# Moving the marks behind which a gathered expert sum may run, in a two-layer backbone with product-key experts

## The chip, the cores and the metric

The kernel runs on one core of one Trainium2 chip. The metric is device time in microseconds (us) of one execution, as the median of several runs. The engines are called PE (TensorE, the matrix engine), PEld (its weight loads), DVE (VectorE), ACT (ScalarE), POOL (GpSimd) and SP (the queue that issues most loads).

## What is computed

Two layers run over one block of 128 context tokens and two blocks of 128 latent tokens. Each layer has a mixer (two kinds of attention and a gated MLP) and then PEER, a layer of 128 x 128 = 16384 experts of one neuron each. This is the part that matters here, cut from the reference:

```python
def one(xb):                                   # 128 tokens
    ...
    top, pos = lax.top_k(cand, PEER_TOPK)      # 8 heads x 16 experts for each token
    idx = jnp.take_along_axis(cidx, pos, axis=-1)
    g = jax.nn.softmax(top.astype(jnp.float32), axis=-1).astype(xb.dtype)
    a = jax.nn.gelu(jnp.einsum('thkd,td->thk', u_tab[idx], xb))
    return jnp.einsum('thk,thkd->td', g * a, v_tab[idx])
```

A token picks 128 experts. For each it needs one row of the table U (1024 numbers; a dot product with the token) and one row of the table V (1024 numbers; added with a weight).

## The kernel before, in words

The kernel computes PEER in two ways at once. For the 256 **latent** tokens it goes densely through both tables on PE. For the 128 **context** tokens it gathers rows. The two share DVE, the DMA engines and the time.

**The dense stages**, one after the other in each layer, for the latent tokens:

- A: `a_step` 0 to 31. Each loads two U tiles (128 experts each, 512 KB), splits most of them into a high and a low part (high on ACT, line 846; low on DVE, line 847, `ulo`), multiplies them with the tokens (line 852) and writes the activations into a large array AR.
- W, the first gate half: 32 `w_step`s. Each builds one-hot matrices for 8 tokens on DVE (lines 876, 878, 883) or ACT (872, 874), multiplies them on PE (line 890, `psW`) and scales AR with the product on DVE (line 897). After every second one there is an `a_step` (32 to 47).
- B: sixteen times one `o_step` (0 to 15) and one `a_step` (48 to 63). An `o_step` loads two V tiles, splits AR (ACT line 906, DVE line 907, `pp`) and mostly also the V tiles (ACT line 915, DVE line 916, `vlo`), and adds the products to four accumulators on PE (line 926, `acc`).
- X, the second gate half: 32 `w_step`s for the other 64 groups of experts, and after every second one an `o_step` (16 to 31); of these, ten of sixteen don't split their V tiles.
- O: `o_step` 32 to 63, all split. Each needs the gates of X for all its tokens, so the first waits for the last write to AR in X.

`U` and `V` tiles come through a ring of six buffers, loaded by SP in program order (line 157); the split parts have two buffers each (pool `w`, `WB = 2`).

**The gathered steps** for the context tokens: 256 in each layer, made in `ctx_gathers`. Steps 0 to 127 are `u_step`s: POOL gathers 128 rows of U with an indirect DMA (line 686, 512 KB, four buffers `gt` in turn), and DVE multiplies and sums them (line 692). Steps 128 to 255 are `v_step`s: POOL gathers rows of V, and DVE adds them to a running sum (line 703; step 128 itself is on line 701). When the last one is done, `ctx_close` normalises the context tokens. In layer 0 their next layer begins there (projection `psic`, line 262); in layer 1 they are written out (line 719).

**Order.** The program is written in the order above, but a scheduler places the instructions of each engine by a simulated timeline and by priority, earlier code first; the order on each engine is then fixed in the program. The gathered steps are written last, so they fill what is free. They would be placed too early where that hurts, so each one is put behind a mark with `tc.issue_after`: its DVE instruction may not be placed ahead of the marked DVE instruction. The gather on POOL has no mark; it waits for its buffer, which DVE frees four steps earlier. Marks are collected by stage: L (top-16 lists of the router), A, W, B, X and O. A mark of A or B is the DVE split of one U tile (line 847), a mark of W or X the first one-hot comparison of one `w_step` (line 878), a mark of O the split of one V tile (line 916). There are 32 marks in L, 40 in A, 32 in W, 32 in B, 32 in X and 64 in O, in each layer. `RATES` says how many steps one mark lets go, `N0` how many steps at the start have no mark:

```python
hold = []
for k, r in RATES[l].items():
    ms = marks[k]
    n = int(len(ms) * r + 0.5)
    hold += [ms[int(i / r)] for i in range(n)]
for j, f in enumerate(ctx_gathers(l, pk)):
    if j < N0[l] or j - N0[l] >= len(hold):
        f()
    else:
        with tc.issue_after(hold[j - N0[l]].ins):
            f()
```

So before the change, in layer 0, 50 steps are free, 8 are let go on L, 56 on A, none on W, 64 on B, 32 on X, and the remaining 46 on O; in layer 1 these are 60, 4, 49, 0, 76, 16 and 51.

Of the kernel before, what the change touches and what calls it, by code (L numbers as in the profile page):

```python
# [45 lines left out]
def tile_fn(ctx: ExitStack, tc, A, outs):  # L46
# [703 lines left out]
    for l in range(DEPTH):  # L750
# [45 lines left out]
        with ExitStack() as es_:  # L796
# [199 lines left out]
# [3 lines that stand above are left out]
# [21 lines left out]
BK = [dict(m=1,s=2,t=2,o=1)]*2  # L1020
PK2 = 'mm'
CQ = 0
RATES = [{'L':0.25,'A':1.4,'W':0.01,'B':2,'X':1,'O':2.125}, {'L':0.125,'A':1.225,'W':0.01,'B':2.375,'X':0.5,'O':2.625}]
N0 = [50,60]
MB = 5
ORD1 = 'paollllllllllllll'
# [96 lines left out]
```

## Time and profile before

| what | us |
|---|---|
| median of 3 runs | 2407.3 (2402.37 to 2410.01) |
| the profiled execution | 2407.9 |
| its span in the trace | 2406.1 |
| PE busy | 2260.6 (94%) |
| DVE busy | 1904.6 (79%) |
| ACT busy | 1115.2 (46%) |
| POOL busy | 697.7 (29%) |
| gathered steps on DVE, lines 692 and 703 | 309.5 and 325.5 |

The span is what the trace covers from the first to the last instruction; the execution's time has a little around it. Busy shares are averages over stages with different limits, so the stage must be looked at before a share means something. Times within the trace count from the start of the span. In this execution the stage B of layer 0 runs from about 725 to 905 us, X to about 1045, O to about 1238; in layer 1 B runs from about 1890 to 2077, X to about 2214 and O to about 2390.

### The profile page before, as it was taken

What the parts mean: (1) busy time and instruction counts of PE and PEld (TensorE: products, weight loads), DVE (VectorE), ACT (ScalarE), POOL (GpSimd) and SP (SyncE); (2) the same over time, 40 slices, a digit from 0 to 9 for tenths busy, and PEclk for the clock granted to TensorE, in tenths of its full rate; (3) what the DMA queues carried; (4) which work ended last, traced back from release to release, by engine and by line L of the source; (5) the groups of instructions that cost most, each with busy time, mean ns of one, the idle gap of its engine ahead of it and who ended that gap; (6) DMA issues with size and microseconds to landing.
All of it is one profiled execution on the core that took longest, in us unless ns stands there. A gap on an engine that the chain in (4) does not pass through costs nothing.

```text
span 2406.1 us, 41658 instructions
## 1 busy us (share of the span) xinstructions
PE 2260.6 (94%) x15660; PEld 1914.5 (80%) x15660; DVE 1904.6 (79%) x3942; ACT 1115.2 (46%) x2084; POOL 697.7 (29%) x523
## 2 busy tenths in 40 slices
PE   6999889999999999999989996989999999998997
PEld 5686469999998995667778785889999889855886
DVE  3157579996898888898863468899879888899987
ACT  3324532442785445444445553134348744444444
POOL 0000233454004433464200003435530143344630
PEclk8999989999999999999999998999999999998998
DMA  9967889999658999999863355989985599987994
GB/s 331 322 193 265 336 322 348 324 358 350 219 159 295 360 332 347 328 352 374 299 213 113 120 158 196 325 313 349 363 320 159 188 374 346 333 309 270 395 364 147
DMA packets 196314, 696.05 MB, mean 289 GB/s; under 512 B 22992, under 2 KB 27408, under 8 KB 196112
## 3 DMA queue, kind: packets, MB, share of 16 engines
q1 hardware_dynamic: 110016, 398.52, 46.7%
q0 software_dynamic: 74736, 272.14, 31.1%
q10 hardware_dynamic: 11360, 22.73, 2.8%
q8 instruction: 123, 2.02, 0.3%
q14 instruction: 79, 0.65, 0.1%
HBM read 689.14 MB, written 4.16 MB: 288 GB/s over the span
## 4 chain that ended last, share of the span: by engine, by line
PE 32%; DVE 8%; issue 8%; DMA 2%; POOL 1%; ACT 1%; DVEq 0%; ACTq 0%; POOLq 0%
PE acc L926 18%; PE psA L852 6%; DVE gt L692 2%; PE psil L262 2%; DMA gt<-in_peer_u_dram,ids 1%; POOL gt L686 1%; PE psqp L561 1%; PE psic L262 1%; DVE ulo L847 1%; PE psoc L522 1%; PE pssl L421 1%; DMA wic<-in_w_in_dram 1%; PE psW L890 0%; DVE idx L550 0%; DVE rep L548 0%
## 5 line engine op out<-in xcount | busy, mean ns | idle before, releaser
L686 POOL DMA_INDIRECT gt<-in_peer_u_dram,ids x256 | 325.3, 1271 | 1185.6 <-DVE gt L692 478.4
L686 POOL DMA_INDIRECT gt<-in_peer_v_dram,ids x256 | 368.0, 1438 | 464.0 <-DVE acc L703 434.7
L926 PE MATMUL acc<-vhi,pp 128*128 128x512 f32 x1728 | 441.9, 398 | 15.6 <-ACT pp L906 9.4
L852 PE MATMUL psA<-h2hi,uhi 128*128 128x256 f32 x1664 | 416.2, 287 | 5.1 <-ACT uhi L846 5.1
L852 PE MATMUL psA<-h2lo,uhi 128*128 128x256 f32 x1664 | 411.3, 284 | 0.0
L926 PEld LDWEIGHTS acc<-vhi,pp 128*128 128x128 f32 x1728 | 326.1, 191 | 86.3 <-ACT pp L906 10.0
L915 ACT ACTIVATE vhi<-v 128x1024 fp32r<-128x1024 f32 x216 | 228.7, 1060 | 274.0 <-PE acc L926 161.2
L692 DVE SCALAR_TENSOR_TENSOR gt<-gt,h2c 128x1024 f32<-128x1024 f32 x256 | 309.5, 1216 | 28.0 <-DMA gt<-in_peer_u_dram,ids 27.9
L703 DVE SCALAR_TENSOR_TENSOR acc<-gt,wcol,acc 128x1024 f32<-128x1024 f32 x254 | 325.5, 1282 | 6.2 <-DMA gt<-in_peer_v_dram,ids 5.2
L846 ACT ACTIVATE uhi<-u 128x1024 fp32r<-128x1024 f32 x208 | 220.0, 1058 | 230.2 <-PE psA L852 107.5
L852 PEld LDWEIGHTS psA<-h2hi,uhi 128*128 128x128 f32 x1664 | 319.7, 192 | 7.9 <-ACT uhi L846 5.7
L852 PEld LDWEIGHTS psA<-h2lo,uhi 128*128 128x128 f32 x1664 | 320.0, 192 | 2.1
L847 DVE TENSOR_TENSOR ulo<-u,uhi 128x1024 fp32r<-128x1024 f32 x208 | 254.3, 1223 | 79.9 <-ACT uhi L846 74.7
L916 DVE TENSOR_TENSOR vlo<-v,vhi 128x1024 fp32r<-128x1024 f32 x216 | 263.6, 1223 | 52.6 <-ACT vhi L915 47.7
L852 PE MATMUL psA<-h2hi,ulo 128*128 128x256 f32 x1664 | 239.4, 286 | 1.0 <-DVE ulo L847 0.8
L926 PE MATMUL acc<-vlo,pp 128*128 128x512 f32 x864 | 234.3, 392 | 1.5 <-DVE vlo L916 1.4
L852 PEld LDWEIGHTS psA<-h2hi,ulo 128*128 128x128 f32 x1664 | 216.2, 192 | 3.0 <-DVE ulo L847 1.6
L872 ACT ACTIVATE e<-iota,nid 128x128 f16<-128x128 f16 x512 | 158.9, 426 | 112.1 <-PE psW L890 112.1
L926 PEld LDWEIGHTS acc<-vlo,pp 128*128 128x128 f32 x864 | 162.3, 189 | 35.8 <-DVE vlo L916 2.5
L852 PE MATMUL psA<-h2T,u 128*128 128x256 f32 x768 | 171.8, 379 | 0.0
L852 PEld LDWEIGHTS psA<-h2T,u 128*128 128x128 f32 x768 | 143.1, 190 | 18.1
L926 PE MATMUL acc<-v,AR 128*128 128x512 f32 x320 | 143.6, 599 | 0.0
(437 smaller groups left out, 3039.9 us busy)
## 6 DMA issues: line engine op xcount, KB each, us to landing
u<-in_peer_uT_dram SPq DMA_DIRECT2D x256, 512.0 KB, 6.0
v<-in_peer_v_dram SPq DMA_DIRECT2D x256, 512.0 KB, 6.0
wm<-in_w_mod_dram SPq DMA_DIRECT2D x96, 512.0 KB, 7.2
wq<-in_peer_wq_dram SPq DMA_DIRECT2D x64, 512.0 KB, 4.7
wic<-in_w_in_dram SPq DMA_DIRECT2D x26, 512.0 KB, 5.7
wil<-in_w_in_dram SPq DMA_DIRECT2D x26, 512.0 KB, 4.2
woc<-in_w_o_dram SPq DMA_DIRECT2D x16, 512.0 KB
wol<-in_w_o_dram SPq DMA_DIRECT2D x16, 512.0 KB, 3.6
```

The source lines that it names most:

```text
L262: T.matmul(ps[:, :n], lhsT=ch.hT[b][:, c, :], rhs=wv[:, c, :], start=(c == 0), stop=(c == 7))
L421: T.matmul(sb[i][:, m * nk:(m + 1) * nk], lhsT=lhs(i, h), rhs=rhs(h), start=True, stop=True)
L686: nc.gpsimd.indirect_dma_start(out=t, out_offset=None, in_=tab, in_offset=bass.IndirectOffsetOnAxis(ap=pk.ids[:, j:j + 1], axis=0))
L692: V.scalar_tensor_tensor(t, t, 1.0, pk.h2c, op0=OP.mult, op1=OP.mult, accum_out=acol[:, j:j + 1])
L703: V.scalar_tensor_tensor(pk.acc, t, wcol[:, j:j + 1], pk.acc, op0=OP.mult, op1=OP.add)
L846: S.activation(hi, ua, AF.Copy)
L847: marks["A" if ii < NA else "U" if ii < NA + PRE else "B"].append(V.tensor_sub(lo, ua, hi.bitcast(F32)))
L852: T.matmul(ps[:, a * 256:(a + 1) * 256], lhsT=lw[:, c * 128:(c + 1) * 128], rhs=rw[:, c, :], start=(k == 0), stop=(k == len(passes) - 1))
L872: S.activation(e2[:, t // TI, :, t % TI], iota1, AF.Abs, bias=nb_[:, t0 % 128 + t:t0 % 128 + t + 1])
L915: S.activation(hi, v, AF.Copy)
L916: marks["O" if ii >= NA else "Q" if ii >= NA - PRE else "P"].append(V.tensor_sub(lo, v, hi.bitcast(F32)))
L926: T.matmul(accp[tb][h], lhsT=pl[:, tb * 128:(tb + 1) * 128], rhs=vr[:, h * 512:(h + 1) * 512], start=st0, stop=sp)
```

## The change

One line changes. In layer 0 a mark of B lets 2.25 steps go instead of 2, one of X 0.5 instead of 1, one of O 2.25 instead of 2.125. In layer 1 it is 2.5 instead of 2.375 in B, 0.01 instead of 0.5 in X, which rounds to none for 32 marks, and 2.75 instead of 2.625 in O.

```diff
-RATES = [{'L':0.25,'A':1.4,'W':0.01,'B':2,'X':1,'O':2.125}, {'L':0.125,'A':1.225,'W':0.01,'B':2.375,'X':0.5,'O':2.625}]
+RATES = [{'L':0.25,'A':1.4,'W':0.01,'B':2.25,'X':0.5,'O':2.25}, {'L':0.125,'A':1.225,'W':0.01,'B':2.5,'X':0.01,'O':2.75}]
 N0 = [50,60]
```

By the loop above this makes, in layer 0, 72 steps let go on B, 16 on X and the remaining 54 on O; in layer 1 80 on B, none on X and the remaining 63 on O.

## Rows read from the trace of the kernel before

**Rows 1.** The page, busy time of each engine with its share of the span.

```profile
PE 2260.6 (94%) x15660; PEld 1914.5 (80%) x15660; DVE 1904.6 (79%) x3942; ACT 1115.2 (46%) x2084; POOL 697.7 (29%) x523
```

**Rows 2.** Stages: from:to, length, busy PE, PEld, DVE, ACT, POOL, clock, DMA, GB/s.

```profile
905.00:1058.00 153.00, 142.08 (x936) 89.23 (x935) 139.25 (x206) 71.21 (x152) 63.39 (x49) 0.97 0.92 333
...
2060.00:2215.00 155.00, 143.92 (x934) 95.13 (x933) 138.32 (x203) 75.65 (x158) 61.75 (x45) 0.95 0.85 306
2215.00:2395.00 180.00, 175.93 (x767) 145.06 (x765) 160.46 (x159) 83.10 (x94) 75.39 (x45) 0.98 0.84 312
```

**Rows 3.** Line 703 on DVE by stretch: length, busy (steps), clock, DMA share, GB/s.

```profile
770.00:1050.50 280.50, 108.52 (x85) 0.98 0.94 341
1107.00:1190.00 83.00, 26.98 (x22) 0.98 0.93 344
...
1943.00:2077.30 134.30, 51.15 (x40) 1.00 0.97 351
2077.30:2164.00 86.70, 29.52 (x23) 1.00 0.88 318
2164.00:2219.40 55.40, 24.22 (x19) 0.82 0.77 272
2219.40:2283.00 63.60, 29.87 (x24) 1.00 1.00 383
2283.00:2362.00 79.00, 28.12 (x22) 1.00 0.94 346
```

**Rows 4.** Timeline of DVE, layer 1, the splits of O's second and third V tile.

```profile
2184.99 1.22 DVE L916 TENSOR_TENSOR vlo<-v,vhi 128x1024 fp32r<-128x1024 f32 x1
...
2219.55 1.22 DVE L916 TENSOR_TENSOR vlo<-v,vhi 128x1024 fp32r<-128x1024 f32 x1
```

**Rows 5.** Short stretches: the end of X in both layers, and two for comparison.

```profile
1025.00:1055.00 30.00, 24.61 (x158) 15.94 (x157) 29.18 (x40) 11.47 (x24) 15.58 (x14) 0.89 0.88 313
...
1910.00:1925.00 15.00, 15.00 (x105) 13.45 (x105) 12.91 (x19) 9.35 (x16) 7.50 (x7) 1.00 0.96 357
...
2165.00:2180.00 15.00, 15.00 (x104) 9.15 (x103) 13.22 (x19) 5.51 (x14) 9.39 (x8) 1.00 0.94 358
2195.00:2225.00 30.00, 18.92 (x168) 15.16 (x167) 27.81 (x44) 15.28 (x33) 11.59 (x11) 0.66 0.62 195
```

**Rows 6.** Line 703 in the burst ending X, and DVE's last write to AR there.

```profile
2195.00:2213.00 18.00, 5.15 (x4) 0.62 0.51 162
...
2212.63 0.77 DVE L897 SCALAR_TENSOR_TENSOR AR<-psW,AR 128x256 f32<-128x256 f32 x2
```

**Rows 7.** The end of the first gate half, where no gathered step runs, both layers.

```profile
710.00:740.00 30.00, 26.69 (x269) 24.81 (x267) 26.74 (x47) 23.52 (x50) 4.01 (x3) 0.94 0.47 144
1880.00:1910.00 30.00, 24.84 (x241) 22.85 (x240) 25.66 (x45) 21.10 (x42) 3.32 (x2) 0.89 0.37 117
```

**Rows 8.** Line 926 alone, O of layer 1: length, busy PE, PEld, clock, DMA, GB/s.

```profile
2215.00:2219.00 4.00, 4.00 (x11) 3.09 (x10) 0.50 0.74 227
2227.00:2231.00 4.00, 4.00 (x20) 3.30 (x19) 1.00 0.99 378
```

**Rows 9.** The context projection at the end of layer 0's O, and PE around it.

```profile
1222.48 3.73 PE L262 MATMUL psic<-wic,hT 128*128 128x128 f32 x32
...
1237.85 3.73 PE L262 MATMUL psic<-wic,hT 128*128 128x128 f32 x32
...
1235.00:1265.00 30.00, 22.06 (x174) 20.38 (x172) 19.86 (x47) 13.16 (x41) 0.00 (x0) 1.00 0.60 183
```

**Rows 10.** Timeline of SP's queue, the last 70 us: start, length, what.

```profile
2338.01 32.97 SPq L157 DMA_DIRECT2D v<-in_peer_v_dram  x13
2378.11 0.35 SPq L719 DMA_DIRECT2D out_dram<-x  x1
2400.92 1.53 SPq L995 DMA_DIRECT2D out_dram<-xl  x2
```

**Rows 11.** DMA issues from 2200 us on: the gathers' median us to landing.

```profile
gt<-in_peer_v_dram,ids POOLq DMA_INDIRECT x49, 7.9
```

## The prediction

> **What bounds the kernel now.** I read the page's busy line first [rows 1]: TensorE (PE) works in 2260.6 of 2406.1 us, 94%, so whatever the change brings can only come out of the 6% in which PE stands still. Then I cut the trace into stages [rows 2]. The second gate half (X) leaves PE idle for 153.0 - 142.1 = 10.9 us in layer 0 and 155.0 - 143.9 = 11.1 us in layer 1, while VectorE (DVE) is busy for 139 us and 138 us of them. The O stage of layer 1 leaves 4 us, most of it before its first matmul.
>
> Third, the gathered V steps are counted by stretch [rows 3]; a step is one DVE instruction of 51.15 / 40 = 1.28 us. Step 128 opens the V steps and is on another line, so 129 + 40 = 169 steps of layer 1 are done at 2077.3 us, where the last mark of B passes. By then the code has let go 60 + 4 + 49 + 76 = 189. The steps run 20 behind their marks, and the rates of B bind only at its start. They bind again late in X: O's first two marks pass by 2185, its third only at 2219.6 [rows 4]. The first o_step's V tiles are split ahead of time, and the second must wait until the first has freed its buffers.
>
> Fourth, where X's idle time lies [rows 5]: before 2195 PE is full (15.00 of 15 us from 2165 to 2180), and all 11.1 us of layer 1 fall between 2195 and 2225. In layer 0 30.0 - 24.6 = 5.4 us fall between 1025 and 1055; the rest of its 10.9 lies earlier, among steps that B holds. In the burst at the end of X nothing is left for PE but the last gate steps, each waiting for DVE; four gathered steps (5.15 us) sit in DVE's queue between 2195 and 2213, and PE starts on O only after the last write to AR (2212.63) [rows 6].
>
> **What the change does to the order.** The same 256 steps, gathers and bytes remain in each layer; only the marks behind which DVE may run them differ. By the code, layer 1 lets go 60 + 4 + 49 + 80 = 193 steps up to B's end, none on X, and six on O's first two marks: 199 by 2219.4, where 169 + 23 + 19 = 211 now stand. So 12 steps (15.4 us of DVE) leave X for O. In layer 0 it is 50 + 8 + 56 + 72 + 16 + 5 = 207 against 129 + 85 = 214: 7 steps, 9.0 us. The faster B rates move at most two or three steps forward at B's start; PE is full there while DVE works for 12.9 of 15 us (1910 to 1925) [rows 5], so DVE has room for one of them in each 15 us behind PE's work, and I cost that at nothing; with that cover gone they would cost 3 x 1.28 = 4 us, given back later.
>
> **Gain at the end of X.** With 9 us of DVE freed ahead of the burst and up to four steps out of it, about three gate steps finish under PE's earlier work. The idle time will not go to nothing: the first half's end, where no gathered step runs, still idles for 30.0 - 26.7 = 3.3 us (710 to 740) and 30.0 - 24.8 = 5.2 us (1880 to 1910) [rows 7]. I take their middle, 4.2. Layer 1 gives 11.1 - 4.2 = 6.9 us. After the pause PE runs at the lower of its two clock levels, 1.2 GHz: 11 matmuls from 2215 to 2219 against 20 later in as long, at a granted clock of 0.50 against 1.00 [rows 8], a loss of 4 x 9 / 20 = 1.8 us. The first half's ends lose clock too (0.94 and 0.89 over 30 us), so I count half, 0.9. Layer 0 gives 5.4 - 4.2 = 1.2 by the same rule; at most two steps leave its short burst, 2.6 us; I take 2. Gain: 6.9 + 0.9 + 2 = about 10 us. Bounds: 0, if the order at the end of X stays, and 11.1 + 5.4 + 2 x 1.8 = 20.
>
> **Given back: the hand-over to layer 1.** Context tokens may start layer 1 only when the last gathered step of layer 0 is done. Their projection starts at 1222.5 and has two blocks of about 3.6 us inside O's matmuls, which end at 1237.85 [rows 9]; alone, O would end near 1230.7, so there are 8 us of slack. In O a step takes 63.6 / 24 = 2.65 us early and 83.0 / 22 = 3.8 us late [rows 3], so seven steps come out 19 to 26 us later, 11 to 18 beyond the slack. Of this PE takes back up to 30.0 - 22.06 = 7.9 us, which it now loses between 1235 and 1265 waiting for this projection's weights [rows 9], and later pauses take more, as the latent chain isn't held. I take 4; ends 0 and 14.
>
> **Given back: the end of the kernel.** Layer 1's last step starts at 2360; its output leaves at 2378.1, the latents' at 2400.9 [rows 10]. That is 23 us of slack for 12 steps. At late O's 79.0 / 22 = 3.6 us they would need 43 us. But SP has issued its last V load at 2371, so some nine of them run against free DMA queues with four buffers at 7.9 us from issue to landing [rows 11], 2 us a step: 3 x 3.6 + 9 x 2 = 29, 6 over. Part of the closing chain fits beside the latents' one. I take 3; ends 0 and 20. O itself is costed at nothing: PE runs full there with 2.65 us per step [rows 3]; if V tiles came late, the cover would be gone and every further step would cost PE its share of the DMA time.
>
> The gathers follow their buffers: POOL's next one waits for DVE to free the fourth one back, so POOL carries the delay and nothing else queues behind it. On SP's queue nothing moves, but X's DMA share (0.85) falls and O's (1.00 early) has no room [rows 2, 3].
>
> **Sum.** -10 + 4 + 3 = -3 us against the profiled execution's 2407.9 (span 2406.1 and 1.8 around it); the median of the runs, 2407.3, is 0.6 below that. Forecast 2405. About 0.3%, 7.2 us, is what a measurement of this kernel can tell from no change.
>
> **Rivals.**
> *Little is given back* (the steps catch up in O, whose DVE is free for a tenth of the time): -10 to -16, 2394. For it: all the hand-over's pauses and the free queues after 2371. Against: late O's slow rate.
> *The steps end too late.* Place: the last steps of O. Price: 14 at the hand-over plus 10 of its 20 us at the end, less a gain of 10 to 15: +9 to +14, 2418. It decides where the last step of layer 0 starts after some 1205 instead of 1188, or layer 1's output leaves after the latents'. For it: early O has DMA at 1.00 [rows 3].
> *The change doesn't do what it says*: the steps lag so far that rates hardly bind and the order stays: 2407. Against: 12 steps can't run before 2219 by the code.
> *X is not bound by PE at all*: every step taken out shortens X by its DVE time, (12 + 7) x 1.28 = 24 us, less 7 given back: 2391. For it: weight loads are busy for only 95 of X's 155 us [rows 2]. Against: PE has no gap from 2165 to 2180, with weight loads at 9.15 of 15 [rows 5]. The Trainium skill, Trainium Kernel Development and Optimization, section Best Practices, has a rule on this side: judge TensorE by the share of weight loads, not by matmul busy time. By that rule X would have over a third to give; the trace disagrees, since full stretches and pauses are cleanly apart.
>
> **How the numbers follow.** Forecast 0.45 (its own range 2399 to 2411: faster 0.08, same 0.37); little given back 0.22, faster; X not bound by PE 0.04, faster; nothing moves 0.08, same; too late 0.21, slower. Together: faster 0.08 + 0.22 + 0.04 = 0.34, same 0.37 + 0.08 = 0.45, slower 0.21. The range runs from 2391 (gain 17, nothing given back) to 2417 (gain 8, 17 given back), which leaves out about one in ten at either end.
>
> **What would show it.** Right: steps done by the third O mark of layer 1 about 199 instead of 211; X's last 30 us with PE idle for 4 to 6 us instead of 11; last steps some 20 us nearer to O's end in both layers; the context projection of layer 1 starting at or after O's last matmul. Wrong: the burst as long as before (gain missed), PE gaps inside O that wait for V tiles (the cover gone), or a context output that leaves last (the tail undersized).

## The result and the profile after

The changed kernel takes 2435.42 us (median of 4 runs, 2434.95 to 2438.18) against 2406.79 for the kernel before on the same chip (4 runs, 2402.37 to 2410.01): ratio 1.0118, interval 1.0098 to 1.0138. It is slower by 1.2%, where 2405 was forecast and 2391 to 2417 was the range. The profiled execution took 2435.45 us, its span is 2433.7, 27.6 us longer than before.

Busy time hardly moved. From the page of the changed kernel, answering to [rows 1]:

```profile
PE 2273.0 (93%) x15660; PEld 1922.7 (79%) x15660; DVE 1900.7 (78%) x3934; ACT 1119.8 (46%) x2092; POOL 693.7 (29%) x523
```

PE is busy for 12.4 us more with the same 15660 matmuls (the same work at a lower mean granted clock, 0.961 against 0.972), and the rest of the 27.6 us is idle time. Where it lies, from the times of a few landmarks in both traces:

| stretch | before | after | difference |
|---|---|---|---|
| start to B's first U split, layer 0 | 732.7 | 734.5 | +1.8 |
| B and X, layer 0 | 311.9 | 313.8 | +1.9 |
| X's last sum of layer 0 to the first U split (line 847) of layer 1 | 527.8 | 539.7 | +11.9 |
| that split to B's first split, layer 1 (A and W) | 331.3 | 336.2 | +4.9 |
| B and X, layer 1 | 309.7 | 308.7 | -1.0 |
| O, layer 1 | 177.5 | 176.3 | -1.2 |
| O's last matmul to the end | 15.2 | 24.5 | +9.3 |

So B and X of layer 1, where most of the gain was looked for, gave one microsecond, those of layer 0 lost two (B 2.7 longer, X 0.7 shorter), and three places away from them took 26. Each column is one trace: the first row alone lies between 733 and 741 us in runs told below in which nothing ahead of B was changed, so a few microseconds in one row are no finding by themselves.

The steps moved as the code says. Line 703 by stretch in the changed kernel, columns as in [rows 3]; the stretches end at the same landmarks as there:

```profile
770.00:1053.50 283.50, 99.74 (x78) 0.98 0.92 335
1110.00:1216.00 106.00, 35.76 (x28) 0.97 0.94 348
...
1964.00:2098.10 134.10, 51.11 (x40) 1.00 0.96 350
2098.10:2184.00 85.90, 28.87 (x23) 1.00 0.88 323
2184.00:2238.00 54.00, 9.47 (x8) 0.87 0.56 193
2238.00:2301.00 63.00, 30.68 (x24) 1.00 0.95 365
2301.00:2418.00 117.00, 42.12 (x33) 0.98 0.86 311
```

In layer 0, 129 + 78 = 207 steps are done at O's third mark (214 before), in layer 1 129 + 40 + 23 + 8 = 199 (211 before). The last 54 us before layer 1's third mark of O hold 8 steps instead of 19. Both counts were forecast to the step.

What X of layer 1 made of it, columns as in [rows 2]:

```profile
2080.00:2235.00 155.00, 144.86 (x943) 96.15 (x942) 128.96 (x195) 76.27 (x158) 50.58 (x37) 0.96 0.79 284
```

DVE works 129 us in X instead of 138, and PE is idle for 10.1 us instead of 11.1. Nearly all of the freed DVE time became idle DVE time.

### The profile page after: what moved, and what is told of

The parts are those of the page before. It is cut to its first block, busy times and chain, and to the rows that moved or that the text cites. A ratio compares the mean times of both kernels' runs of the same rounds, so it can differ in the third digit from the quotient of the medians.

```text
span 2433.7 us, 41645 instructions
## 1 busy us (share of the span) xinstructions
PE 2273.0 (93%) x15660; PEld 1922.7 (79%) x15660; DVE 1900.7 (78%) x3934; ACT 1119.8 (46%) x2092; POOL 693.7 (29%) x523
## 5 line engine op out<-in xcount | busy, mean ns | idle before, releaser
L686 POOL DMA_INDIRECT gt<-in_peer_u_dram,ids x256 | 314.4, 1228 | 894.1 <-DVE gt L692 485.7
L686 POOL DMA_INDIRECT gt<-in_peer_v_dram,ids x256 | 375.0, 1465 | 518.1 <-DVE acc L703 476.6
```

Of the source, the lines that this page charges most:

```text
L686: nc.gpsimd.indirect_dma_start(out=t, out_offset=None, in_=tab, in_offset=bass.IndirectOffsetOnAxis(ap=pk.ids[:, j:j + 1], axis=0))
```

## Why X gained nothing, read from the two traces

The waits of PE over 21 us around the end of X in layer 1 (from 2195 and from 2215), first the kernel before (engine, what waited, for whom: us, times, longest):

```profile
PE psW L890 <- DVE e L883: 6.6, 4, 1.8
PE psW L890 <- ACT e L874: 2.7, 2, 1.5
PE acc L926 <- ACT pp L906: 1.8, 1, 1.8
```

then the changed kernel:

```profile
PE psW L890 <- ACT e L874: 6.8, 3, 2.9
PE psW L890 <- DVE e L883: 2.2, 2, 1.6
PE acc L926 <- ACT pp L906: 1.2, 1, 1.2
```

The pause is nearly as long, and another engine is last. ACT builds the first one-hot of every second gate step (lines 872 and 874, 3.5 us together), three of them in the burst. ACT's timeline there (start, length, in brackets the idle time before and who ended it), first the kernel before:

```profile
2197.01 2.49 ACT L872 ACTIVATE e<-iota,nid 128x128 f16<-128x128 f16 x8 [3.48 <-PE psW L890]
...
2209.32 1.06 ACT L874 ACTIVATE e<-e 128x1024 f16<-128x1024 f16 x1
```

then the changed kernel:

```profile
2218.33 2.48 ACT L872 ACTIVATE e<-iota,nid 128x128 f16<-128x128 f16 x8 [6.41 <-PE psW L890]
...
2222.70 2.48 ACT L872 ACTIVATE e<-iota,nid 128x128 f16<-128x128 f16 x8 [0.81 <-PE psW L890]
...
2229.97 1.06 ACT L874 ACTIVATE e<-e 128x1024 f16<-128x1024 f16 x1
```

From the first to the last of them ACT takes 13.4 us before and 12.7 us after: without the gathered steps this chain is hardly shorter. What PE did ahead of it in the changed kernel:

```profile
2211.60 5.31 PE L926 MATMUL acc<-v,AR 128*128 128x512 f32 x12
2216.75 1.13 PE L890 MATMUL psW<-e,e 128*128 128x64 f16 x32
```

ACT stood idle for 6.4 us until PE released a one-hot buffer. A one-hot has two buffers (pool `X`). PE works off 5.31 us of an `o_step` first and only then the gate steps that hold them; after that six gate steps follow one another through two buffers, each in turn waiting for PE, while PE has 0.7 to 1 us of work in each. DVE isn't free there either, though no gathered step is left in the burst; its time is the third figure with a count:

```profile
2217.44:2229.40 11.96, 4.68 (x95) 4.00 (x91) 11.55 (x27) 9.01 (x25) 0.39 (x1) 0.73 0.49 187
```

The gate steps alone keep it busy for 11.55 of 11.96 us. So taking four gathered steps out of DVE's queue leaves a chain through ACT, DVE and the buffers that is nearly as long. The experiments below that change who builds the one-hots, and how many buffers they have, test this reading.

## The experiments

Each ratio is against the kernel before, measured side by side on the same chip, with its 95% interval. "Last step" is the start of a layer's last gathered step.

**One layer at a time.** The new rates in layer 0 alone (layer 1 as before), then in layer 1 alone.

```diff
-RATES = [{'L':0.25,'A':1.4,'W':0.01,'B':2,'X':1,'O':2.125}, {'L':0.125,'A':1.225,'W':0.01,'B':2.375,'X':0.5,'O':2.625}]
+RATES = [{'L':0.25,'A':1.4,'W':0.01,'B':2.25,'X':0.5,'O':2.25}, {'L':0.125,'A':1.225,'W':0.01,'B':2.375,'X':0.5,'O':2.625}]
```

```diff
+RATES = [{'L':0.25,'A':1.4,'W':0.01,'B':2,'X':1,'O':2.125}, {'L':0.125,'A':1.225,'W':0.01,'B':2.5,'X':0.01,'O':2.75}]
```

> Layer 0 has the new rates, layer 1 the old ones. Theory 1 (the gathered steps end too late: 26 us later in layer 0, so the context tokens start layer 1 late; separately the closing chain of layer 1 runs behind the latents'): only the hand-over's share is paid, some 18 us, about 2425; last step of layer 0 at about 1214, first context projection near 1245, the output of the context tokens out before the latents'. Theory 2 (the cost comes from the changed order in layer 1's B, X and O): about 2407. Theory 3 (the steps' end doesn't matter, B and O are slowed by denser steps): a third to a half of the 28 us, 2416 to 2421, with B or O of layer 0 longer.

> Layer 1 has the new rates, layer 0 the old ones. Theory 1: only the tail is paid, 9 us, less about 1 us won at the end of X: about 2415; layer 1 begins as in the kernel before (first context projection near 1222) and the context output leaves last. Theory 2 (changed order in layer 1): nearly the whole, about 2432. Theory 3: 2414 to 2420 with a longer B or O of layer 1.

Layer 0 alone: 2423.57 us, 1.0055 (1.0038 to 1.0071). Layer 1 alone: 2421.92, 1.0046 (1.0026 to 1.0066). The two ratios multiplied give 1.0101, the whole change within its interval. With layer 0 alone the hand-over is that of the changed kernel (538.0 us from X's end to the first U split) and the tail that of the kernel before (15.2); with layer 1 alone it is 528.4 and 24.5. So the two costs are separate, one in each layer, and neither layer's X pays for them.

**Which half of the edit.** X's rates lowered alone, then B's and O's raised alone.

```diff
+RATES = [{'L':0.25,'A':1.4,'W':0.01,'B':2,'X':0.5,'O':2.125}, {'L':0.125,'A':1.225,'W':0.01,'B':2.375,'X':0.01,'O':2.625}]
```

```diff
+RATES = [{'L':0.25,'A':1.4,'W':0.01,'B':2.25,'X':1,'O':2.25}, {'L':0.125,'A':1.225,'W':0.01,'B':2.5,'X':0.5,'O':2.75}]
```

> Only the two X rates are lowered, B and O keep the old rates. Theory 1: as slow as the whole change or slower, since fewer steps are let go ahead of O: 2435 to 2445. Theory 3 (denser B and O): about 2407.

> Only the B and O rates are raised, X keeps the old rates. Theory 1: as before or a little faster, 2402 to 2410, since the steps run behind their marks and end no later. Theory 3: slower, 2420 to 2435.

X alone: 2454.59 us, 1.0193 (1.0172 to 1.0213). Last steps at 1240.5 and 2438.8, both behind O's last matmul (1227.3 and 2422.4); the hand-over takes 559.1 and the tail 29.9 us. B and O alone: 2417.77, 1.003 (1.0016 to 1.0045), where no difference was expected: the hand-over takes 522.4 us, but A and W of layer 1 336.8 instead of 331.3. So the raised rates win back some of what the lowered X costs, and are no gain by themselves. In this run the two stretches named cancel; where its 0.3% lies is not shown.

**The same rates with an earlier start.** Seven and twelve more steps without a mark, so that the lag at the end is made up at the beginning.

```diff
-N0 = [50,60]
+N0 = [57,72]
```

> All new rates, but 57 and 72 steps without a mark instead of 50 and 60, so 7 and 12 more steps are let go ahead of each later mark: 214 and 211 by O's third mark, as in the kernel before, while X still has its few. Theory 1 (the cost is the late end of the steps): the whole cost goes, within 6 us of the kernel before on the same chip, with last steps near 1190 and 2360. Theory 2 (thinner X or denser B and O cost by themselves): still 15 to 28 us slower than before.

2424.43 us, 1.0047 (1.003 to 1.0065). Steps at O's third mark are 214 and 211 again, hand-over (524.3) and tail (15.2) as before: this part was right. But A and W of layer 1 take 347.5 us, 16 more. The U steps that don't find a place in A run on into W, as the count of line 692 there shows (a step leaves two records), from the kernel before, the changed one and this one:

```profile
1780.20:1885.00 104.80, 4.98 (x8) 1.00 0.58 187
```

```profile
1796.30:1908.00 111.70, 12.23 (x20) 0.98 0.64 209
```

```profile
1789.40:1910.00 120.60, 27.02 (x44) 0.97 0.73 250
```

4, 10 and 22 steps in W go with 331.3, 336.2 and 347.5 us for A and W: 0.8 to 0.9 us for each on average (the first few come cheaper: in the next run 6 steps go with 331.7 us). So the cost of lateness moved from the end to W instead of going away.

**The late steps left out.** The new rates without the last 7 V steps of layer 0 and the last 12 of layer 1 (their terms are missing from the context tokens' sums).

```diff
-        return [lambda j=j: u_step(j) for j in range(128)] + [lambda j=j: v_step(j) for j in range(128)]
+        return [lambda j=j: u_step(j) for j in range(128)] + [lambda j=j: v_step(j) for j in range(128 - (7, 12)[l])]
```

> All new rates, and the last 7 (layer 0) and 12 (layer 1) gathered V steps are left out, so the context tokens' sums lack those experts. Theory 1: the steps end about where they did before, the hand-over and the tail cost nothing: within 6 us of the kernel before. Theory 2: the time falls by no more than the steps' own DVE time where DVE is the limit, a few us, and stays 15 us or more above before.

2410.67 us, 0.9993 (0.9978 to 1.0008). Last steps at 1189.0 and 2362.6, hand-over 524.1, tail 15.2: every cost is gone, so it was the lateness. And still nothing is gained, with X as the new rates make it: the missing gain is X's own.

**Steps let go in W.** With the new rates, 7 and 12 marks of W let steps go; then, with the old rates, 8 in each layer.

```diff
+RATES = [{'L':0.25,'A':1.4,'W':0.22,'B':2.25,'X':0.5,'O':2.25}, {'L':0.125,'A':1.225,'W':0.375,'B':2.5,'X':0.01,'O':2.75}]
```

```diff
+RATES = [{'L':0.25,'A':1.4,'W':0.25,'B':2,'X':1,'O':2.125}, {'L':0.125,'A':1.225,'W':0.25,'B':2.375,'X':0.5,'O':2.625}]
```

> All new rates, and 7 and 12 steps are let go on the marks of the first gate half (W), where the queues have room (DMA share 0.5 to 0.6 there) and PE is full. Theory 1: as the run with the earlier start, the late end goes: within 6 us of before; W itself is longer by at most 2 to 4 us, as DVE is busy for nine tenths there. Theory 2: still 15 us or more slower.

> The old rates, and 8 steps of each layer let go on W. Theory 1 says where time is still to be had: the steps of layer 0 end some 20 us earlier, the context projection starts earlier under O, and of the 8 us that PE loses between 1235 and 1265 some come back; layer 1's tail stays, as the latents end last: 2 to 8 us faster than before. If W pays more for the steps than the hand-over gives, 0 to 6 us slower.

New rates: 2424.41 us, 1.0049 (1.0032 to 1.0066); hand-over 525.8, tail 15.2, but A and W of layer 1 take 340.3 and those of layer 0 334.8 (328.0 before), 0.75 to 1 us for each step put into W. Old rates: 2450.63, 1.0168 (1.0148 to 1.0188), with the steps *earlier* than in the kernel before: last step of layer 0 at 1166.6, hand-over 562.9 us. Earliness costs too, here 35 us at the hand-over. That was not foreseen.

**Four steps fewer in the kernel before.** To see that effect by itself, the kernel before without the last 4 V steps of layer 0 (their terms are missing from the sums).

```diff
+        return [lambda j=j: u_step(j) for j in range(128)] + [lambda j=j: v_step(j) for j in range(128 - (4, 0)[l])]
```

> The kernel before with the last four gathered V steps of layer 0 left out, so less work. Theory 1a (the context projection is the filler of the pause between O's last matmul and the latents' first projection, and pays on both sides: late it leaves the pause empty, early it takes PE from O): the projection starts some 15 us earlier, O ends some 7 to 11 us later, and the time rises by 3 to 10 us. Theory 1b (an earlier end of the steps only helps): 0 to 8 us faster.

2423.84 us, 1.0051 (1.0031 to 1.0071): less work, 12 us slower. PE's timeline of this run (first, fourth and fifth block of the context projection, and what follows O's last `acc`):

```profile
1215.73 3.73 PE L262 MATMUL psic<-wic,hT 128*128 128x128 f32 x32
...
1243.16 3.73 PE L262 MATMUL psic<-wic,hT 128*128 128x128 f32 x32
...
1251.75 0.61 PE L926 MATMUL acc<-vlo,pp 128*128 128x512 f32 x2
1252.21 3.73 PE L262 MATMUL psic<-wic,hT 128*128 128x128 f32 x32
1258.14 5.44 PE L262 MATMUL psic<-wic,hT 128*128 128x128 f32 x32 [2.20 <-ACT la_y L115]
```

and of the changed kernel:

```profile
1232.87 1.07 PE L926 MATMUL acc<-vlo,pp 128*128 128x512 f32 x4
1240.43 1.97 PE L201 MATMUL m1pst<-ident,m1xh 128*128 128x128 f32 x8 [6.49 <-DVE m1xh L147]
1245.19 6.13 PE L262 MATMUL psic<-wic,hT 128*128 128x128 f32 x32 [2.79 <-DVE hT L207]
```

The context projection is the only work that the traces show on PE between O's last matmul and the latents' first one (the latents' closing chain on DVE lies between). Started early, it is spent between O's matmuls, where PE was full anyway: counted from X's last sum, O ends after 202.5 us instead of 193.4, and the latents, which set the end, come later. Started late, it isn't there when the gap opens: PE waits 6.49 + 2.79 us, and the first block runs at the lower clock, 6.13 us instead of 3.73.

These are the largest pieces of the hand-over's cost, but not its account: the kernel before paused at this place too, for the projection's weights, and without the projection's blocks the changed kernel's O is 7.8 us shorter. From X's last sum of layer 0 to layer 1's first U split, first before, then after, columns as in [rows 2]:

```profile
1044.60:1572.40 527.80, 484.55 (x2826) 406.89 (x2827) 378.06 (x941) 231.11 (x501) 118.27 (x87) 0.96 0.68 236
```

```profile
1048.30:1588.00 539.70, 491.06 (x2830) 414.68 (x2831) 371.85 (x924) 234.48 (x509) 115.78 (x83) 0.93 0.66 227
```

PE is idle for 48.6 us instead of 43.2 and busy for 6.5 us longer with the same work, at a granted clock of 0.93 instead of 0.96. Over half of the 11.9 us is the same work at a lower clock.

The runs so far give a curve: how long before O's last matmul the last step of layer 0 starts, and what lies between X's end and layer 1's first U split.

| run | before O's end | hand-over, us |
|---|---|---|
| old rates, W marks | 98.6 | 562.9 |
| four steps fewer | 71.2 | 541.0 |
| late steps left out | 52.7 | 524.1 |
| layer 1 alone | 50.7 | 528.4 |
| kernel before | 49.6 | 527.8 |
| new rates, W marks | 49.6 | 525.8 |
| earlier start | 46.1 | 524.3 |
| B and O alone | 44.0 | 522.4 |
| layer 0 alone | 19.8 | 538.0 |
| changed kernel | 19.7 | 539.7 |
| X alone | -13.2 | 559.1 |

Between 53 and 44 us it is flat within 6 us; on either side it rises. The runs told further down fit: 523.7 to 527.7 us in five of them, between 52.8 and 31.6 us before O's end, and 537.0 and 537.9 in two at 17.5. The first column isn't independent of the second on the early side, since the projection itself puts O's end off there (by 21 us in the first row and 9 in the second).

**A third buffer for the projection's weights** in the kernel before, for the 7.9 us in which [rows 9] shows PE waiting behind O.

```diff
-            cring.tile([128, 1024], F32, name=name, tag="cring", bufs=2)
+            cring.tile([128, 1024], F32, name=name, tag="cring", bufs=3)
```

> The kernel before with three buffers instead of two for the context weights of layer 1. Theory 1a: the waits of PE for these weights in the pause (6.4 us between 1225 and 1290) mostly go, and the latents' first projection is not delayed: 2 to 6 us faster than before. If the pause is set by the latents' chain alone: no change.

2408.5 us, 0.9985 (0.9975 to 0.9995). PE at the same place, columns as in [rows 5]:

```profile
1242.00:1272.00 30.00, 26.82 (x221) 25.30 (x219) 20.25 (x55) 17.10 (x54) 0.00 (x0) 1.00 0.74 221
```

The idle time falls from 7.9 to 3.2 us, and the kernel is faster by 0.15%, which the interval just tells from nothing.

**ScalarE out of the burst.** The changed kernel with the last eight gate steps' one-hots on DVE.

```diff
-                if frac(n, EA):
+                if frac(n, EA) and not (hf == 1 and n >= 24):
```

> All new rates, and the last eight gate steps of X build their one-hots on DVE alone. Theory A (in the new order DVE is free at the end of X and PE waits for the one-hots that ACT builds): PE's idle time at the end of layer 1's X falls from 10.1 us to about 5, that of layer 0 from 4.3 to about 3, and the time by 4 to 8 us against the changed kernel, to about 2428. Theory B (the pause is the length of the chain of the last gate steps, whoever builds them): idle time 9 us or more there, 2432 to 2440.

2431.36 us, 1.0084 (1.0065 to 1.0103). PE waits for ACT's one-hots no more, but 7.4 us for DVE's; its last 30 us of X, and then the burst in them:

```profile
2210.00:2240.00 30.00, 21.38 (x175) 16.17 (x174) 23.85 (x44) 4.73 (x6) 6.49 (x5) 0.72 0.38 135
```

```profile
2214.20:2227.40 13.20, 5.75 (x105) 4.88 (x102) 13.20 (x30) 0.00 (x0) 0.94 (x1) 0.61 0.40 154
```

8.6 us idle instead of 10.1. DVE is idle for 6 of the 30 us, but not in the burst: there it works for 13.20 of 13.20 us. With ACT's share on it, DVE is the bound, so the idle time of neither theory came (about 5, or 9 and more). The ratio is 0.3% below the changed kernel's, about as theory A had it, but 1.5 us of idle time don't account for that, and the two intervals touch.

**More work left for PE.** The kernel before with the third weight buffer and with X's `o_step`s issued three later, so that three are left for the end.

```diff
-                if (n + 1) * PRE // NW > n * PRE // NW:
-                    o_step(NA - PRE + n * PRE // NW)
+                if (n + 1) * PRE // NW > n * PRE // NW and n * PRE // NW >= LAG:
+                    o_step(NA - PRE + n * PRE // NW - LAG)
...
-            for ii in range(NA, 2 * NA):
+            for ii in range(NA - LAG, 2 * NA):
...
+LAG = 3
```

> The kernel before with a third buffer for the weight blocks of the context projection (as in the run before) and with the multiplications of X's steps issued three steps later, so that three of them are left behind the last gate steps. Theory, the pause at X's end is TensorE having no multiplication left while the last gate steps run on the other engines: its idle time over the 30 us behind X's last sum falls from 11.1 to about 4 us in layer 1 and from 5.4 to about 3 us in layer 0, and the ratio is 0.993 to 0.996, against 0.9985 for the third buffer alone. Rival, the pause only moves, or the gathered steps end at another place and the hand-over gives the gain back: idle in the two stretches together falls by less than 3 us, or the first psic block moves by more than 3 us against O's last sum, and the ratio is 0.998 to 1.010.

2412.98 us, 1.0007 (0.9991 to 1.0024): the rival's figure. PE's last 30 us of X in layer 1, and PE's timeline around the burst:

```profile
2204.00:2234.00 30.00, 18.55 (x170) 14.89 (x169) 27.39 (x43) 15.49 (x33) 10.99 (x11) 0.72 0.62 197
```

```profile
2198.50 6.25 PE L926 MATMUL acc<-v,AR 128*128 128x512 f32 x14
...
2222.59 3.78 PE L926 MATMUL acc<-vhi,pp 128*128 128x512 f32 x8 [1.75 <-ACT pp L906]
```

11.4 us idle. But the experiment did not test its theory in layer 1. The edit moves the `o_step`s in the program's text, and the scheduler placed them on PE where they had been (in the kernel before these two lines are the same, at 2189.69 and 2213.78): in both, all 688 matmuls of line 926 that layer 1 does up to X's end stand ahead of the last eight gate steps, and nothing is left for the burst. In layer 0 the order did change, and PE's idle time at X's end fell from 5.4 to 4.6 us. Whether multiplications left for the burst would fill it is not shown.

**A third one-hot buffer.** That left the two buffers. To make room, the modulation's row was put into its bias tile and the weights of the gathered sum into the tile of its activations (first diff, the control); then came one more buffer for the first one-hot of a gate step, which ACT builds in every second one (second diff), with the old and with the new rates.

```diff
-        row = sm.tile([128, 256], F32, name="modrow", tag="modrow", bufs=1)
+        row = bm
-        wcol = cp.tile([128, 128], F32, name="wcol", tag="wcol")
+        wcol = acol
```

```diff
-                e2 = X.tile([128, G, 128, TI], F16, name="e2", tag="e2")
+                e2 = X.tile([128, G, 128, TI], F16, name="e2", tag="e2", bufs=3)
```

> Control: the kernel before with two pairs of small tiles sharing their memory (the modulation's row with its bias, the weights of the gathered sum with its activations), nothing else. Both theories: TensorE's idle time at the end of X stays at 11 (layer 1) and 5.4 us (layer 0), and the ratio is 0.997 to 1.003.

> The control with a third buffer for the first one-hot of a gate step (the one that ScalarE builds for every other step). Theory, the pause is a chain through the two one-hot buffers: ScalarE can start one step earlier, so that its wait for TensorE before the first of the last three (3.5 us in the kernel before) goes, the idle time at the end of X falls by 3 to 6 us in layer 1 and by 1 to 3 in layer 0, and the ratio against the control is 0.997 to 0.998. Rival, VectorE's own work sets the pause (it is busy for 27.8 of the last 30 us): idle stays within 1.5 us of the control's, and so does the time.

> The changed kernel with the same shared tiles and the third one-hot buffer. Theory, with VectorE relieved of the gathered steps and the buffers no longer holding ScalarE, the pause falls below that of the run before this: to 4 to 6 us in layer 1 from 10.1 in the changed kernel, so X of layer 1 is 4 to 6 us shorter than in the changed kernel; the time stays 1.005 to 1.010 above that of the kernel before, for the steps still end late. Rival: idle stays at 8.5 us or more.

Control: 2417.0 us, 1.0028 (1.0008 to 1.0047), with a longer pause at the end of layer 0's X, which was not expected; the third buffer with the old rates: 2404.77, 0.9974 (0.9961 to 0.9986), against the control 0.995; with the new rates: 2425.57, 1.0066 (1.0046 to 1.0087). PE's last 30 us of X in layer 1, first the old rates with the third buffer, then the new rates with it, then the changed kernel with two:

```profile
2190.00:2220.00 30.00, 19.43 (x160) 14.43 (x157) 28.93 (x44) 14.41 (x32) 14.72 (x13) 0.72 0.76 251
```

```profile
2198.00:2228.00 30.00, 23.46 (x182) 16.97 (x182) 22.04 (x39) 15.07 (x33) 7.30 (x6) 0.83 0.48 174
```

```profile
2215.00:2245.00 30.00, 19.86 (x178) 15.79 (x177) 21.36 (x39) 15.47 (x33) 5.88 (x5) 0.77 0.38 131
```

| end of X, layer 1: PE idle, us | two one-hot buffers | three |
|---|---|---|
| old rates (gathered steps in the burst) | 11.1 | 10.6 |
| new rates (none) | 10.1 | 6.5 |

In these four traces only both together shorten it by more than 1 us. With the old rates and three buffers DVE's queue is the wait (all 8.8 us of PE's waits on one-hots are for DVE's), and the expected 3 to 6 us did not come in layer 1. With the new rates and two buffers it is ACT behind the buffer; the third one gives 3.6 us, and B and X take 305.1 us instead of 308.7, a little less than the 4 to 6 expected. With three buffers PE's last piece of an `o_step` stands ahead of six gate steps, with two ahead of eight. This is how a wait with two covers behaves: taking one off shows the other. But other runs scatter by as much as one cover seems to hide: with two buffers and X's rates lowered alone it is 8.1 us, with three buffers and the old rates 8.4 in the run below. So one change alone is worth 0.5 to 3 us, and the 4.6 us of both rest on one trace. In layer 0 the figures tell nothing: 5.4 us in the kernel before, 11.8 in the control, and with three buffers 3.4, 5.1 (new rates) and 5.7 (the run below). The Trainium skill, Perfetto Trace Analysis, section Identifying Performance Opportunities, says that the same gap coming back on the engine that should be full can mean too little memory for the next tile, by the count of buffers; the trace agrees here, once DVE is out of the way, with those 3.6 us of 10.1.

The third buffer serves both gate halves, so these runs also bear on W. W and what follows it up to B's first U split, in layer 1, with 10 gathered steps in W in both, first the changed kernel, then the new rates with the third buffer:

```profile
1796.40:1924.20 127.80, 119.38 (x1317) 116.39 (x1316) 115.99 (x209) 101.05 (x205) 13.21 (x12) 0.96 0.59 194
```

```profile
1788.20:1911.00 122.80, 118.25 (x1338) 114.78 (x1337) 116.80 (x212) 102.61 (x214) 13.12 (x12) 1.00 0.62 203
```

That is 5 us less for the same steps, and more than the buffer gave in X. W of layer 0, which has no gathered step, takes 120.6 and 119.9 us in the two runs, so ten steps cost 7.2 us with two buffers and 2.9 with three. Much of what a gathered step costs in W goes with the buffers too.

**Both buffers**, in the kernel before with the old rates.

> The kernel before with the shared small tiles, the third one-hot buffer and the third buffer for the weight blocks of the context projection. If the two gains are separate they add: 0.9974 x 0.9985 = 0.996 against the kernel before. If the third one-hot buffer already moved the context projection behind O, so that the pause between the weight blocks lies elsewhere, the third weight buffer adds nothing: 0.997 to 0.998.

2400.45 us, 0.9951 (0.9935 to 0.9967): the gains add, as far as the interval tells, and this version beats both kernels. The hand-over takes 524.8 us, and X's end in layer 1 idles for 30.0 - 21.56 = 8.4:

```profile
2176.00:2206.00 30.00, 21.56 (x179) 15.26 (x178) 28.61 (x46) 14.74 (x33) 14.45 (x12) 0.83 0.76 245
```

## Why the prediction was wrong, step by step

**Right.** The count of steps at O's third mark (207 and 199), the direction of the last steps (forecast some 20 us nearer to O's last matmul, measured 30 in layer 0 and 38 in layer 1), the context projection behind O's last matmul, and O costing nothing. What happened is the rival that the steps end too late, whose point of decision was a last step of layer 0 after some 1205 (it starts at 1214.2) and a context output behind the latents' (2429.8 against 2424.1 and 2426.8). It had its place right and its price too low, 2418 for 2435.

**Gain at the end of X: 10 forecast, about 1 in layer 1 and none in layer 0 measured.** The step that failed is "with 9 us of DVE freed ahead of the burst and up to four steps out of it, about three gate steps finish under PE's earlier work". All four steps did leave it (none in the last 16 us). But none of the gate steps moved ahead: they pass through two one-hot buffers that PE holds, and the chain through ACT took 12.7 us instead of 13.4. [rows 5] had DVE busy for 27.8 of 30 us there, and I took a busy engine for the cause without asking what PE would wait for next. ACT's wait before its first one-hot was in the trace of before as well (3.48 us). My lower bound of 0 held as a number, but not for its reason: the order at the end of X did change. A reading beside it was wrong too: the 4 us that PE is idle in [rows 2] from 2215 to 2395 lie behind O's last matmul, which ends at 2390.9, and not before its first.

**The faster B rates: nothing forecast, 2.7 in layer 0 measured.** "I cost that at nothing; with that cover gone they would cost 3 x 1.28 = 4 us": in layer 0 the cover was gone once. Behind the first marks of B, DVE waited 3.75 us in all for four gathers ahead of a V split, and PE for the split:

```profile
758.24 1.85 PE L926 MATMUL acc<-vlo,pp 128*128 128x512 f32 x4 [3.06 <-DVE vlo L916]
```

In layer 1 B is 0.6 us longer.

**Hand-over: 4 forecast, 11.9 and 4.9 measured.** PE did take back most of what it lost waiting for this projection's weights, from the end of O to 1300, first before, then after:

```profile
PE psic L262 <- DMA wic<-in_w_in_dram: 6.4, 5, 2.0
```

```profile
PE psic L262 <- DMA wic<-in_w_in_dram: 1.0, 2, 0.5
```

What failed is the price of the delay "11 to 18 beyond the slack", which was netted with this to 4. Behind O a pause of 9.3 us stands in place of the weights' waits, in which PE has nothing but eight transposes, and the whole stretch runs at a lower clock, for 6.5 us more of PE's time; the sum had no term for the clock here. The slack of 8 us was counted to O's last matmul, which was the right place; the upper end, 14, holds the 11.9. The 4.9 us have no term either: layer 1's gathered steps start 33 us later (1511.5 instead of 1478.1), six more of them fall into W, and W pays 0.8 us for each.

**Tail: 3 forecast, 9.3 measured.** "Nine of them run against free DMA queues ... 2 us a step" was mis-sized, and the cause it names isn't the one that binds. Behind the last V load the steps take 28.5 / 10 = 2.85 us:

```profile
2389.50:2418.00 28.50, 12.60 (x10) 0.93 0.51 168
```

DVE waits for no gather in these last steps; all its waits from 2385 to 2420:

```profile
DVE vlo L916 <- ACT vhi L915: 2.5, 3, 1.3
DVE y L990 <- PE acc L926: 0.8, 1, 0.8
```

Most of the steps stand in DVE's fixed order between the V splits and so go at the pace at which PE takes the V tiles, whatever the DMA queues could do. The last three stand in DVE's queue between the pieces of the latents' closing chain, and then the context tokens' own chain shares DVE with it. DVE's timeline:

```profile
2413.24 1.28 DVE L703 SCALAR_TENSOR_TENSOR acc<-gt,wcol,acc 128x1024 f32<-128x1024 f32 x1
2414.44 1.22 DVE L991 SCALAR_TENSOR_TENSOR y<-xr,y 128x1024 f32<-128x1024 f32 x1
...
2416.77 1.27 DVE L703 SCALAR_TENSOR_TENSOR acc<-gt,wcol,acc 128x1024 f32<-128x1024 f32 x1
```

and the outputs leave in the other order than in [rows 10]:

```profile
2424.11 3.00 SPq L995 DMA_DIRECT2D out_dram<-xl  x2
2429.75 0.33 SPq L719 DMA_DIRECT2D out_dram<-x  x1
```

**The other rivals.** That X is not bound by PE and gets shorter by each microsecond of DVE taken out fell: 12 steps left layer 1's X, and B and X together are 1.0 us shorter. That little is given back fell with the hand-over.

**What stays open.** Why W takes longer for each gathered step in it (0.75 to 1 us for a 1.2 us instruction, with DVE not full) is shown in part only: the third one-hot buffer takes 5 us off W with ten steps in it, and what the rest waits for was not taken apart. How much the end of X could give with work left for PE in the burst is open, since the run that was to show it left PE's order in layer 1 as it was. The fall of the hand-over's curve between 71 and 53 us has only those two points.

## What to carry to other kernels

Before you price the removal of work from a busy engine, ask what the waiting engine would wait for then: a pause can have two covers (a full queue and a buffer that is not free), and taking one off then gives little. Work that has slack at both ends (here the projection of a second chain) is worth most where the main engine has nothing else; being early costs too, so look for the stretch it should fill, not for the earliest start. Deferred work is given back at the places where its end is waited for, and each of these needs its own price, with the shift carried on to the next stage.

## What the runs showed that was not expected

Less work made the kernel slower: without four gathered steps (5 us of DVE) it took 12 us longer, since the order of PE changed with the moment at which the context chain became free. The same holds for edits of the program's text: three `o_step`s written later stayed where they were on PE in layer 1, because the scheduler places them by its own timeline.

After 9.3 us of idle time in two pieces PE came back at the lower of its two clock levels (1.2 GHz): the first block of 32 matmuls of the projection took 6.13 us instead of 3.73, with a granted clock of 0.50 from 1237 to 1249 and of 0.77 over the 30 us from 1225:

```profile
1225.00:1255.00 30.00, 20.29 (x108) 17.71 (x106) 24.10 (x47) 13.57 (x34) 0.00 (x0) 0.77 0.45 138
```

A pause costs more than its length: here 2.4 us on top of 9.3.
